# A float32 matmul with bias and residual: row order of the first tiles, paired first loads, the bias by a shuffle, and filler matmuls

## The chip, the core and the metric

The kernel runs on one core of one Trainium2 chip. The core has a matrix engine (TensorE, PE in the profile, with its weight loads as PEld), a vector engine (VectorE, DVE), a scalar engine (ScalarE, ACT), GpSimd (POOL) and a sync engine (SyncE, SP), which here only issues transfers. Sixteen DMA engines carry the transfers between the chip's memory (HBM) and the core's SBUF; each transfer over 128 partitions is split over all sixteen, eight partitions each. The metric is the device time of one execution in microseconds, lower is better.

## The reference

```
x: 16 x 512 x 1024, weight: 1024 x 768, bias: 768, residual: 16 x 512 x 768, all float32
out = matmul(x, weight) + bias + residual
```

Flattened, this is one product of 8192 x 1024 by 1024 x 768. It reads 33.6 MB of x, 25.2 MB of residual and 3.1 MB of weight, and writes 25.2 MB.

## The kernel before, in words

**Tiles and groups.** The 8192 rows are 64 tiles of 128 rows, and four tiles make a group (`G = 4`, 16 groups). A group's rows can lie on the 128 partitions in two ways, which `group` decides. For groups 1 to 15 partition p holds rows 4p to 4p + 3, so that a partition's share of x is one run of 16 KB in memory, and of residual or output one run of 12 KB. For group 0 tile j is rows 128j to 128j + 127, so each row is a run of its own (4 KB of x, 3 KB of residual and output). A row may be in any tile as long as the residual and the output follow the same order, and they do, since all three go through `group`. The weight is kept in two halves of four pieces, and piece k (128 of the 1024 inner rows) is one row per partition, 3 KB.

**One tile.** `cast_x` makes bf16 of the tile, whole on ACT (L124) or, in the first stage, half on ACT (L121) and half on DVE (L122). `transpose` turns its eight 128 x 128 blocks on PE (L140) into a PSUM tile `pt`, `copy_xt` (DVE, L147) brings that to SBUF, `matmul` (L154) makes 16 matmuls, for each of 8 weight pieces one of 512 columns and one of 256, into the PSUM tile `po`. `evacuate` adds: for the first three groups DVE adds the bias into `o_tile` (L169) and POOL adds the residual (L170); later DVE adds the residual in place (L173) and POOL the bias (L175). For the last group the bias is added to the residual ahead of time (`add_bias`, L183). There are three `po` buffers and two `pt` buffers.

**Transfers.** All but the bias are issued by SP, in the order of the program: `load_x` (L96), `load_w` (L101), `load_r` (L105), `store` (L109). At most eight transfers are under way, since eight completion counters go round: each issue waits until the transfer eight places before it has landed. There are four x buffers and a ring of nine buffers shared by weight, residual and output. The bias (one row of 3 KB) is issued by ACT (L81).

**The first stage.** 40 matmuls on a constant tile (`WARM`, L210) come first on PE. Then tiles 0 to 2 are started together, because the weight is still arriving: each weight piece, once it is cast to bf16 (`cast_w`, DVE L131 or ACT L129), is multiplied with all three tiles. The bias is spread to all partitions by a product of a column of ones with the bias row in float32 on PE (L217), copied out by ACT into `bias_bc` (L226). Tile 3 is transposed when the last weight pieces come. The order of issue in this stage is written out by hand, and each engine takes its work in that order (`keep_in_program_order`).

**The loop.** From tile 3 on, each step casts tile t + 3, transposes tile t + 1, multiplies tile t, copies and evacuates. After the last tile of group g SP issues the x and residual of group g + 4 and then the store of group g. The last group is stored in four parts, the last tile as 512 and 256 columns (L285, L288).

Of the kernel before, what the change touches and what calls it, by code (L numbers as in the profile page):

```python
# [8 lines left out]
FP32 = mybir.dt.float32  # L9
BF16 = mybir.dt.bfloat16  # L10
P = 128
G = 4
# [4 lines left out]
PT_BUFS = 2  # L17
PO_BUFS = 3
LATE = 3
WARM = 40  # L20


@with_exitstack
def kernel(
# [8 lines left out]
    nc = tc.nc  # L33
# [4 lines left out]
    N = weight.shape[1]  # L38
# [3 lines left out]
    chunks = [(0, 512), (512, N - 512)]  # L42

    def group(ap, g):
        rows = ap[g * G * P:(g + 1) * G * P, :]


        if g == 0:
            return rows.rearrange("(j p) k -> p j k", p=P)
        return rows.rearrange("(p j) k -> p j k", p=P)  # L50


    w_dram = weight.rearrange("(h p j) n -> h p j n", p=P, j=4)
# [1 line left out]
    const = ctx.enter_context(tc.tile_pool(name="const", bufs=1))  # L55
# [6 lines left out]
    po_pool = ctx.enter_context(  # L62
        tc.tile_pool(name="pop", bufs=1, space=bass.MemoryType.PSUM))

    def o(ins):
        return tc.keep_in_program_order(ins)
# [3 lines left out]
    def slot(pool, base, n, shape, dtype, name=None):  # L70
        i = count.get(base, 0)
        count[base] = i + 1
        return pool.tile(shape, dtype, name=name or base, tag=f"{base}{i % n}", bufs=1)


    warm_in = const.tile([P, P], BF16, name="warm_in")
    o(nc.vector.memset(warm_in, 0.5))  # L77
    ones_row = const.tile([1, P], FP32, name="ones_row")
    o(nc.vector.memset(ones_row, 1.0))
    bias_row = const.tile([1, N], FP32, name="bias_row")  # L80
    o(nc.scalar.dma_start(out=bias_row, in_=bias[None, :]))  # L81
    warm = const.tile([1, 2], FP32, name="warm")
    o(nc.vector.memset(warm, 0.0))
    o(nc.scalar.copy(out=warm, in_=warm))  # L84
# [3 lines left out]
    bias_bc = const.tile([P, N], FP32, name="bias_bc")  # L88
# [4 lines left out]
    def load_x(g, j0=0, j1=G):  # L93
        if g not in x_tiles:
            x_tiles[g] = slot(xin_pool, "x_tile", X_BUFS, [P, G, K], FP32)
        o(nc.sync.dma_start(out=x_tiles[g][:, j0:j1, :], in_=group(x2d, g)[:, j0:j1, :]))  # L96

    def load_w(h, j0, j1):
        if h not in w_stage:
            w_stage[h] = slot(ring_pool, "ring", RING, [P, G, N], FP32, name="w_stage")  # L100
        o(nc.sync.dma_start(out=w_stage[h][:, j0:j1, :], in_=w_dram[h, :, j0:j1, :]))  # L101

    def load_r(g):
        r_tiles[g] = slot(ring_pool, "ring", RING, [P, G, N], FP32, name="r_tile")
        o(nc.sync.dma_start(out=r_tiles[g], in_=group(res2d, g)))  # L105

    def store(g, j0=0, j1=G, n0=0, n1=N):
        src = o_tiles[g] if g < LATE else r_tiles[g]
        o(nc.sync.dma_start(out=group(out2d, g)[:, j0:j1, n0:n1], in_=src[:, j0:j1, n0:n1]))  # L109
# [4 lines left out]
    def cast_x(t, split=False):  # L114
        if t >= n_sub:
            return
        xb_tiles[t] = slot(xb_pool, "xb", XB_BUFS, [P, K], BF16)
        src = x_tiles[t // G][:, t % G, :]
        if split:
            h = K // 2  # L120
            o(nc.scalar.copy(out=xb_tiles[t][:, :h], in_=src[:, :h]))  # L121
            o(nc.vector.tensor_copy(out=xb_tiles[t][:, h:], in_=src[:, h:]))  # L122
        else:
            o(nc.scalar.copy(out=xb_tiles[t], in_=src))  # L124

    def cast_w(k, act=False):
        h, j = divmod(k, 4)
        if act:
            o(nc.scalar.copy(out=w_sb[:, k, :], in_=w_stage[h][:, j, :]))  # L129
        else:  # L130
            o(nc.vector.tensor_copy(out=w_sb[:, k, :], in_=w_stage[h][:, j, :]))  # L131

    def transpose(t):
        if t >= n_sub:
            return
        xb = xb_tiles.pop(t).rearrange("m (h p j) -> m h j p", p=P, j=4)
        pt = slot(pt_pool, "pt", PT_BUFS, [P, n_k, P], BF16)
        for k in range(n_k):
            h, j = divmod(k, 4)
            o(nc.tensor.transpose(out=pt[:, k, :], in_=xb[:, h, j, :], identity=ident))  # L140
        pt_tiles[t] = pt

    def copy_xt(t):
        if t >= n_sub:
            return
        xt_tiles[t] = slot(xt_pool, "xt", XT_BUFS, [P, n_k, P], BF16)
        o(nc.vector.tensor_copy(out=xt_tiles[t], in_=pt_tiles.pop(t)))  # L147

    def matmul(t, k0=0, k1=n_k):
        if t not in po_tiles:  # L150
            po_tiles[t] = slot(po_pool, "po", PO_BUFS, [P, N], FP32)
        for k in range(k0, k1):
            for (n0, nl) in chunks:
                o(nc.tensor.matmul(  # L154
                    po_tiles[t][:, n0:n0 + nl],
                    lhsT=xt_tiles[t][:, k, :],
                    rhs=w_sb[:, k, n0:n0 + nl],
                    start=(k == 0),
                    stop=(k == n_k - 1),
                ))  # L160
# [22 lines left out]
        o(engine.tensor_add(out=rt[:, j, :], in0=rt[:, j, :], in1=bias_bc))  # L183


    load_x(0, 0, 1)
    load_x(0, 1, 2)
    load_w(0, 0, 1)
    load_x(0, 2, 3)
    load_w(0, 1, 2)  # L190
    load_w(0, 2, 3)
    load_w(0, 3, 4)
    load_w(1, 0, 1)
    load_w(1, 1, 2)
    load_w(1, 2, 3)
    load_x(0, 3, 4)
    load_w(1, 3, 4)
    load_x(1, 0, 2)
    load_x(1, 2, 4)
    load_x(2)  # L200
    load_r(0)
    load_x(3)
# [2 lines left out]
    load_r(3)  # L205


    warm_ps = slot(po_pool, "po", PO_BUFS, [P, P], FP32, name="warm_ps")
    for i in range(WARM):
        o(nc.tensor.matmul(warm_ps, lhsT=warm_in, rhs=warm_in, start=True, stop=True))  # L210


    cast_x(0, True)
    transpose(0)
    bias_ps = slot(po_pool, "po", PO_BUFS, [P, N], FP32, name="bias_ps")
    for (n0, nl) in chunks:
        o(nc.tensor.matmul(bias_ps[:, n0:n0 + nl], lhsT=ones_row,  # L217
                           rhs=bias_row[:, n0:n0 + nl], start=True, stop=True))
    slot(po_pool, "po", PO_BUFS, [P, P], FP32, name="unused_ps")
    copy_xt(0)  # L220
    cast_x(1, True)
    transpose(1)
    cast_w(0)
    matmul(0, 0, 1)
    copy_xt(1)
    o(nc.scalar.copy(out=bias_bc, in_=bias_ps))  # L226
    matmul(1, 0, 1)
    cast_x(2, True)
    transpose(2)
# [2 lines left out]
    matmul(0, 1, 2)  # L232
    matmul(1, 1, 2)
    matmul(2, 0, 2)
    for k in range(2, 6):
        cast_w(k, k % 2 == 0)
        for t in range(3):
            matmul(t, k, k + 1)
    cast_w(6)
    cast_x(3, True)  # L240
    transpose(3)
    cast_w(7, True)
    copy_xt(3)
    matmul(0, 6, 7)
    matmul(1, 6, 7)
    matmul(0, 7, 8)
# [9 lines left out]
    for t in range(3, n_sub - 1):  # L256
        g, j = divmod(t, G)
# [24 lines left out]
    for (n0, nl) in chunks:  # L282
        ps = slot(po_pool, "po", PO_BUFS, [P, nl], FP32, name="last_ps")
        for k in range(n_k):
            o(nc.tensor.matmul(ps, lhsT=xt_tiles[t][:, k, :], rhs=w_sb[:, k, n0:n0 + nl],  # L285
                               start=(k == 0), stop=(k == n_k - 1)))
# [31 lines left out]
```

## Time and profile before

| | |
|---|---|
| median of 3 runs | 213.12 us (213.1 to 214.03) |
| the profiled execution | 213.84 us; its span, first to last instruction, 212.1 us |
| PE busy | 202.3 us, 95% of the span |
| DMA queue of SP | 87.04 MB, packets for 97.8% of the time of 16 engines |
| DVE, ACT, POOL busy | 107.4, 65.9, 113.6 us |

Busy times overlap, so their sum means nothing; a busy share of 95% on one engine and of 97.8% on the queue says that both are near their limit, not which of them ends the run. The views used are the page (shares, slices, queues, chain, groups), the waits and the timeline of an engine (start, length, instruction, and in brackets the idle time before it and what ended it), windows (busy time of each engine in a stretch), and the records of the DMA packets (size, start, length of each) and of the completion counters (when each of the sixteen engines reported its part of a transfer), which the trace holds as well.

### The profile page before, as it was taken

The page shows a single profiled execution, that of the slowest core. Times are in us where ns is not written, and L with a number is a line of the kernel's source. Part 1 is how long each engine was busy: PE and PEld are TensorE (multiplying, and loading weights), DVE is VectorE, ACT ScalarE, POOL GpSimd, SP SyncE. Part 2 cuts the span into 40 slices and gives each one's busy share as a digit, 9 for nine tenths or more (in the row PEclk, how much of TensorE's full clock was granted, in tenths as well). Part 3 has the DMA queues.
Part 4 walks back from the last instruction along what each step waited for, and adds up shares of the span by engine and source line. Part 5 has one row for each costly group of instructions (what it writes and reads, how often), then busy time and mean ns, then how long its engine had stood idle before and what let it go on. Part 6 is the DMA issues. An engine that isn't in the chain of part 4 may idle for free.

```text
span 212.1 us, 3712 instructions
## 1 busy us (share of the span) xinstructions
PE 202.3 (95%) x1550; PEld 135.1 (64%) x1580; DVE 107.4 (51%) x143; ACT 65.9 (31%) x70; POOL 113.6 (54%) x68
## 2 busy tenths in 40 slices
PE   8899999999999999999999999999999999999990
PEld 8555666666666666666666666666666666666650
DVE  1556455455545544554455445544554455458750
ACT  3335571411607024070603306070421507042000
POOL 1000009699966556555655565566556655667800
PEclk9889999999999999999999999999999999999998
DMA  6999999999999999999999999999999999999993
GB/s 224 384 414 434 408 429 420 427 430 418 424 428 418 443 420 433 423 431 427 420 432 426 428 426 440 419 425 432 420 432 427 438 416 427 438 414 430 403 401 132
DMA packets 9859, 87.28 MB, mean 412 GB/s; under 512 B 1009, under 2 KB 1137, under 8 KB 4082
## 3 DMA queue, kind: packets, MB, share of 16 engines
q1 hardware_dynamic: 9840, 87.04, 97.8%
q8 instruction: 12, 0.20, 0.4%
q14 instruction: 5, 0.04, 0.0%
q10 hardware_dynamic: 2, 0.00, 0.0%
HBM read 61.87 MB, written 25.17 MB: 410 GB/s over the span
## 4 chain that ended last, share of the span: by engine, by line
PE 90%; DMA 3%; DVE 3%; issue 1%; SPq 0%; DVEq 0%
PE po L154 76%; PE pt L140 13%; DMA w_stage<-in_weight_dram 3%; PE last_ps L285 1%; DVE r_tile L183 1%; DVE xt L147 1%; DVE o_tile L169 0%; SPq L96 0%; DVE w_sb L131 0%; DVE r_tile L288 0%; DVE r_tile L173 0%; DVEq L173 0%; DVEq L169 0%
## 5 line engine op out<-in xcount | busy, mean ns | idle before, releaser
L154 PE MATMUL po<-w_sb,xt 128*128 128x256 bf16 (+1 forms) x978 | 173.1, 325 | 3.0 <-DVE xt L147 0.6
L154 PEld LDWEIGHTS <-xt 128*128 128x128 bf16 x1008 | 96.2, 98 | 60.0 <-DVE xt L147 1.7
L175 POOL TENSOR_TENSOR r_tile<-r_tile,bias_bc 128x768 f32<-128x768 f32 x48 | 88.2, 1838 | 54.8 <-DVE r_tile L173 54.8
L124 ACT CAST xb<-x_tile 128x1024 bf16<-128x1024 f32 x60 | 58.7, 1043 | 115.2 <-DMA x_tile<-in_x_dram 95.3
L173 DVE TENSOR_TENSOR r_tile<-po,r_tile 128x768 f32<-128x768 f32 x51 | 48.8, 957 | 73.6 <-PE po L154 64.3
L147 DVE COPY xt<-pt 128x1024 bf16<-128x1024 bf16 x64 | 43.6, 681 | 4.4 <-PE pt L140 4.4
L140 PEld LDWEIGHTS <-xb 128*128 128x128 bf16 x512 | 35.8, 114 | 8.3 <-ACT xb L121 1.0
L140 PE MATMUL pt<-ident,xb 128*128 128x128 bf16 x512 | 39.6, 221 | 0.0
L170 POOL TENSOR_TENSOR o_tile<-o_tile,r_tile 128x768 f32<-128x768 f32 x12 | 21.4, 1823 | 31.8 <-DMA r_tile<-in_residual_dram 31.8
L169 DVE TENSOR_TENSOR o_tile<-po,bias_bc 128x768 f32<-128x768 f32 x12 | 11.3, 955 | 12.2 <-PE po L154 10.7
L210 PE MATMUL warm_ps<-warm_in 128*128 128x128 bf16 x40 | 4.4, 313 | 1.1 <-DVE warm_in L77 1.1
L210 PEld LDWEIGHTS <-warm_in 128*128 128x128 bf16 x40 | 4.2, 149 | 1.1 <-DVE warm_in L77 1.1
L131 DVE CAST w_sb<-w_stage 128x768 bf16<-128x768 f32 x5 | 2.8, 560 | 3.7 <-DMA w_stage<-in_weight_dram 3.7
L121 ACT CAST xb<-x_tile 128x512 bf16<-128x512 f32 x4 | 2.5, 618 | 5.3 <-DMA x_tile<-in_x_dram 5.3
L122 DVE CAST xb<-x_tile 128x512 bf16<-128x512 f32 x4 | 1.7, 424 | 3.8 <-DMA x_tile<-in_x_dram 3.7
L183 POOL TENSOR_TENSOR r_tile<-r_tile,bias_bc 128x768 f32<-128x768 f32 x2 | 3.6, 1808 | 0.0
L129 ACT CAST w_sb<-w_stage 128x768 bf16<-128x768 f32 x3 | 2.5, 832 | 2.8 <-DMA w_stage<-in_weight_dram 2.8
L183 DVE TENSOR_TENSOR r_tile<-r_tile,bias_bc 128x768 f32<-128x768 f32 x2 | 3.1, 1556 | 0.0
L285 PE MATMUL last_ps<-w_sb,xt 128*128 128x512 bf16 (+1 forms) x16 | 2.8, 326 | 0.0
L285 PEld LDWEIGHTS <-xt 128*128 128x128 bf16 x16 | 1.6, 98 | 1.1
L84 ACT ACT_TABLE_LOAD x1 | 1.3, 1283 | 1.3 <-PEq L302 1.3
L288 DVE TENSOR_TENSOR r_tile<-last_ps,r_tile 128x512 f32<-128x512 f32 (+1 forms) x2 | 1.1, 558 | 0.9 <-PE last_ps L285 0.8
(13 smaller groups left out, 4.5 us busy)
## 6 DMA issues: line engine op xcount, KB each, us to landing
x_tile<-in_x_dram SPq DMA_DIRECT2D x14, 2048.0 KB, 32.8
r_tile<-in_residual_dram SPq DMA_DIRECT2D x16, 1536.0 KB, 32.4
out_dram<-r_tile SPq DMA_DIRECT2D x12, 1536.0 KB, 31.7
out_dram<-o_tile SPq DMA_DIRECT2D x3, 1536.0 KB, 25.8
w_stage<-in_weight_dram SPq DMA_DIRECT2D x8, 384.0 KB, 8.2
x_tile<-in_x_dram SPq DMA_DIRECT2D x4, 512.0 KB, 5.7
x_tile<-in_x_dram SPq DMA_DIRECT2D x2, 1024.0 KB, 10.3
out_dram<-r_tile SPq DMA_DIRECT2D x1, 768.0 KB, 7.5
```

Of the source, the lines that this page charges most:

```text
L124: o(nc.scalar.copy(out=xb_tiles[t], in_=src))
L131: o(nc.vector.tensor_copy(out=w_sb[:, k, :], in_=w_stage[h][:, j, :]))
L140: o(nc.tensor.transpose(out=pt[:, k, :], in_=xb[:, h, j, :], identity=ident))
L147: o(nc.vector.tensor_copy(out=xt_tiles[t], in_=pt_tiles.pop(t)))
L154: o(nc.tensor.matmul(po_tiles[t][:, n0:n0 + nl], lhsT=xt_tiles[t][:, k, :], rhs=w_sb[:, k, n0:n0 + nl], start=(k == 0), stop=(k == n_k - 1),))
L169: o(nc.vector.tensor_add(out=ot[:, j, :], in0=po, in1=bias_bc))
L170: o(nc.gpsimd.tensor_add(out=ot[:, j, :], in0=ot[:, j, :], in1=r_tiles[g][:, j, :]))
L173: o(nc.vector.tensor_add(out=rt, in0=po, in1=rt))
L175: o(nc.gpsimd.tensor_add(out=rt, in0=rt, in1=bias_bc))
L183: o(engine.tensor_add(out=rt[:, j, :], in0=rt[:, j, :], in1=bias_bc))
L210: o(nc.tensor.matmul(warm_ps, lhsT=warm_in, rhs=warm_in, start=True, stop=True))
L285: o(nc.tensor.matmul(ps, lhsT=xt_tiles[t][:, k, :], rhs=w_sb[:, k, n0:n0 + nl], start=(k == 0), stop=(k == n_k - 1)))
```

## The change

Group 0 takes the row order of the other groups. So its x, its residual and its output are runs of 16 KB or 12 KB on a partition, and tiles 0 and 1, and 2 and 3, are loaded as two pairs. Weight pieces 2 and 3, and 4 and 5, are loaded as pairs; group 1 of x is one transfer in place of two. The order of the first transfers is new. The bias row is sent to four partitions (0, 32, 64, 96) of a tile that POOL has set to zero, and a VectorE stream shuffle copies lane 0 of each 32 partitions to all of them; the product with ones and the copy by ACT are gone. Tiles 1 and 3 are cast whole on ACT. Tile 3 is cast, transposed and copied before weight piece 2 is used, no longer after piece 6. `fill(n)` puts n matmuls on the constant tile into PE's order: the 40 at the start, and 10, 6 and 4 more between the first transposes and matmuls; their PSUM tile is the third `po` buffer.

```diff
     def group(ap, g):
-        rows = ap[g * G * P:(g + 1) * G * P, :]
-        if g == 0:
-            return rows.rearrange("(j p) k -> p j k", p=P)
-        return rows.rearrange("(p j) k -> p j k", p=P)
+        return ap[g * G * P:(g + 1) * G * P, :].rearrange("(p j) k -> p j k", p=P)
...
-    ones_row = const.tile([1, P], FP32, name="ones_row")
-    o(nc.vector.memset(ones_row, 1.0))
-    bias_row = const.tile([1, N], FP32, name="bias_row")
-    o(nc.scalar.dma_start(out=bias_row, in_=bias[None, :]))
+    bias_rows = const.tile([P, N], FP32, name="bias_rows")
+    o(nc.gpsimd.memset(bias_rows, 0.0))
+    o(nc.scalar.dma_start(out=bias_rows[0:P:32, :], in_=bias[None, :].to_broadcast([4, N])))
...
-    load_x(0, 0, 1)
-    load_x(0, 1, 2)
+    load_x(0, 0, 2)
     load_w(0, 0, 1)
-    load_x(0, 2, 3)
+    load_x(0, 2, 4)
     load_w(0, 1, 2)
-    load_w(0, 2, 3)
-    load_w(0, 3, 4)
-    load_w(1, 0, 1)
-    load_w(1, 1, 2)
+    load_w(0, 2, 4)
+    load_w(1, 0, 2)
     load_w(1, 2, 3)
-    load_x(0, 3, 4)
     load_w(1, 3, 4)
-    load_x(1, 0, 2)
-    load_x(1, 2, 4)
+    load_x(1)
     load_x(2)
...
-    warm_ps = slot(po_pool, "po", PO_BUFS, [P, P], FP32, name="warm_ps")
-    for i in range(WARM):
-        o(nc.tensor.matmul(warm_ps, lhsT=warm_in, rhs=warm_in, start=True, stop=True))
+    warm_ps = po_pool.tile([P, P], FP32, name="warm_ps", tag="po2", bufs=1)
+    def fill(n):
+        for i in range(n):
+            o(nc.tensor.matmul(warm_ps, lhsT=warm_in, rhs=warm_in, start=True, stop=True))
+    fill(40)
     cast_x(0, True)
     transpose(0)
-    bias_ps = slot(po_pool, "po", PO_BUFS, [P, N], FP32, name="bias_ps")
-    for (n0, nl) in chunks:
-        o(nc.tensor.matmul(bias_ps[:, n0:n0 + nl], lhsT=ones_row,
-                           rhs=bias_row[:, n0:n0 + nl], start=True, stop=True))
-    slot(po_pool, "po", PO_BUFS, [P, P], FP32, name="unused_ps")
+    fill(10)
     copy_xt(0)
-    cast_x(1, True)
+    cast_x(1)
     transpose(1)
+    fill(6)
+    o(nc.vector.stream_shuffle(out=bias_bc, in_=bias_rows, mask=[0] * 32))
     cast_w(0)
     matmul(0, 0, 1)
     copy_xt(1)
-    o(nc.scalar.copy(out=bias_bc, in_=bias_ps))
+    fill(4)
     matmul(1, 0, 1)
     cast_x(2, True)
     transpose(2)
...
     matmul(2, 0, 2)
+    cast_x(3)
+    transpose(3)
+    copy_xt(3)
     for k in range(2, 6):
         cast_w(k, k % 2 == 0)
         for t in range(3):
             matmul(t, k, k + 1)
     cast_w(6)
-    cast_x(3, True)
-    transpose(3)
     cast_w(7, True)
-    copy_xt(3)
     matmul(0, 6, 7)
```

More of the change, by code (lines that the diff above doesn't have):

```diff
@@ L19 @@
 LATE = 3
-WARM = 40
 @with_exitstack
```

## The prediction

> **What bounds the kernel now.** I read the page from the top: engine shares, slices, DMA queues, chain. Two resources come out nearly full, and the page alone does not say which of them ends the run.
>
> ```profile
> PE 202.3 (95%) x1550; PEld 135.1 (64%) x1580; DVE 107.4 (51%) x143; ACT 65.9 (31%) x70; POOL 113.6 (54%) x68
> ...
> PEclk9889999999999999999999999999999999999998
> DMA  6999999999999999999999999999999999999993
> ...
> q1 hardware_dynamic: 9840, 87.04, 97.8%
> q8 instruction: 12, 0.20, 0.4%
> ...
> PE 90%; DMA 3%; DVE 3%; issue 1%; SPq 0%; DVEq 0%
> ```
>
> The chain names PE for 90%, but the one data queue moves packets for 97.8% of the span of all 16 DMA engines, and 0.4% more goes to instruction fetches: 208.3 of 212.1 us on the mean engine. So I looked at who waits for whom at the end, in the timeline of SP's issues, the list of DMA issues and the windows of the tail.
>
> ```profile
> 206.92 0.33 SPq L109 DMA_DIRECT2D out_dram<-r_tile  x1
> ```
>
> ```profile
> out_dram<-r_tile SPq DMA_DIRECT2D x1, 768.0 KB, 7.5
> out_dram<-r_tile SPq DMA_DIRECT2D x1, 384.0 KB, 5.4
> out_dram<-r_tile SPq DMA_DIRECT2D x1, 256.0 KB, 4.5
> out_dram<-r_tile SPq DMA_DIRECT2D x1, 128.0 KB, 4.3
> ```
>
> ```profile
> 199.00:200.00 1.00, 1.00 (x9) 0.61 (x7) 0.41 (x1) 0.00 (x0) 1.00 (x2) 1.00 0.78 332
> 200.00:205.00 5.00, 4.95 (x36) 3.01 (x35) 2.51 (x3) 0.00 (x0) 0.78 (x1) 1.00 0.98 413
> ...
> 207.00:208.00 1.00, 0.00 (x0) 0.00 (x0) 0.00 (x0) 0.00 (x0) 0.00 (x0) 1.00 0.89 345
> 208.00:209.00 1.00, 0.00 (x0) 0.00 (x0) 0.00 (x0) 0.00 (x0) 0.00 (x0) 1.00 0.52 193
> 209.00:210.00 1.00, 0.00 (x0) 0.00 (x0) 0.00 (x0) 0.00 (x0) 0.00 (x0) 1.00 0.23 87
> ```
>
> (Columns of the windows: length, busy PE, PEld, DVE, ACT, POOL, then clock, DMA share, GB/s.) PE is done at 206.4. The last store, 128 KB, is issued at 206.92 and lands 4.3 us later, at 211.2, while the share sinks slowly (0.89, 0.52, 0.23). The DMA engines finish one after another. The landing records of the trace (each of the 16 engines reports its part) say it exactly. The last engine reports the stores of the tail at 203.88, 207.52, 209.34, 210.27, 210.89 and 211.23; these steps of 3.64, 1.82, 0.93, 0.62 and 0.34 are eight packets each at the medians of the packet records (12 KB 460 ns, 6 KB 234, 3 KB 121, 2 KB 84, 1 KB 46: 3.68, 1.87, 0.97, 0.67, 0.37). That engine never waited for data. The end is its backlog, not PE. On the fastest engine the last store landed at 208.59, 1.67 us after issue, and the first load of the run (512 KB, 3.36 us to landing, of which 1.27 is eight 4 KB packets at 159 ns) gives 3.36 - 1.27 + 0.37 = 2.46 us as the other price of a 128 KB store on an empty queue. So PE has 4.3 less 1.67 to 2.46 = 1.8 to 2.6 us of slack at the end.
>
> How near PE is everywhere else shows in the waits of the first stage and the steady state:
>
> ```profile
> 16.49 0.62 ACT L121 CAST xb<-x_tile 128x512 bf16<-128x512 f32 x1 [2.40 <-DMA x_tile<-in_x_dram]
> 17.44 0.83 ACT L129 CAST w_sb<-w_stage 128x768 bf16<-128x768 f32 x1 [0.34 <-DMA w_stage<-in_weight_dram]
> 20.00 1.99 ACT L124 CAST xb<-x_tile 128x1024 bf16<-128x1024 f32 x2 [1.73 <-DMA x_tile<-in_x_dram]
> 22.47 2.00 ACT L124 CAST xb<-x_tile 128x1024 bf16<-128x1024 f32 x2 [0.47 <-DMA x_tile<-in_x_dram]
> ...
> 151.36 3.89 ACT L124 CAST xb<-x_tile 128x1024 bf16<-128x1024 f32 x4 [8.30 <-DMA x_tile<-in_x_dram]
> 163.56 3.89 ACT L124 CAST xb<-x_tile 128x1024 bf16<-128x1024 f32 x4 [8.31 <-DMA x_tile<-in_x_dram]
> ```
>
> Groups of x land every 12.20 us; PE, by the chain, takes 4 x (2.60 + 0.45) = 12.2 us for four tiles; and each first cast of a group ends 2.25 us before its transpose (164.6 against 166.85). PE and DMA run side by side at the same pace, PE a little behind what has landed, the DMA engines never dry.
>
> **The change part by part.**
>
> *Layout, pairs and fewer transfers: DMA time.* This is on the path, since the last DMA engine has no gaps. Each engine moves 8 of a transfer's 128 row pieces; price by the packet medians (also 8 KB 313 ns, 16 KB 611). Tiles of group 0: 32 x 159 = 5.09 becomes 16 x 313 = 5.01. Group 1: 16 x 313 = 5.01 becomes 8 x 611 = 4.89. Weight: 64 x 121 = 7.74 becomes 32 x 121 + 16 x 234 = 7.62. Residual of group 0 and its store, 3 KB pieces now (they too follow the row order): each 32 x 121 = 3.87 becomes 8 x 460 = 3.68. Saved: 0.08 + 0.12 + 0.12 + 0.19 + 0.19 = 0.70. Five transfers fewer (x six to three, weight eight to six), each with a completion write of 9 ns per engine: 0.05. Sum 0.75 us.
>
> The page's list has a transfer landing in 5.7 to 33 us because it stands in a queue, and a transfer's own completion write takes 9 ns. The Trainium skill (DMA: Bandwidth & Descriptors, section "Anatomy of one DMA — SWDGE (gpsimd) path") puts a fixed cost of about 2.0 us on each transfer of the software path; here the hardware path is used, and five fewer would by that rule be 10 us. With the queue full the trace shows none of it, so the rule is left out of the sum.
>
> *Cold packets.* Packets starting before 5 us took 0.60 us per engine more than their medians, those from 5 to 10 us 0.22 us, and the window 4.5 to 6.5 has a DMA share of 0.90, 0.2 us empty. With half as many first packets between 0 and 1.0 us of it could go; between 0 and 0.5 could come, if long packets suffer more. I take 0: it is seen at the first touch of each tensor, which stays.
>
> *First casts, on DVE and ACT.* Tile 0 was cast at 4.12, when its 512 KB had landed, tile 1 at 5.40. Now both come in one transfer: about 5.35. Halves of 0.62 (ACT) and 0.43 (DVE) as before; tiles 1 and 3 are now whole on ACT, 1.04 each, in place of halves.
>
> *Bias.* Removed: two fp32 matmul calls (four recorded, 1.55 us of PE), the copy of 0.80 on ACT. Added: a POOL memset of 128x768 f32; the row 128x128 bf16 took 0.20, six times the columns and twelve times the bytes give 1.2 to 2.4 us. It delays the identity (0.49 on POOL) to 3.6 at most, wanted at 6.0. The bias transfer waits for it on ACT's queue; behind it stand the table load (1.28) and one copy (0.19), done by 5.1 (the issue itself 0.50), before the cast at 5.35. SP's queue is not touched. The shuffle is new; nearest DVE rows of 128x768 are the cast (0.56) and the f32 add (0.95), the dearest 1.56. I take 0.95. It stands before the cast of weight piece 0, which landed at 8.04: DVE idled 0.83 us there. At 1.56 that cast would be 0.7 us later, and pieces 1 to 7 pace PE anyway. It costs nothing on the path. The Trainium skill (VectorE: DVE Perf Modes, "The perf-mode tier table") gives about 2400 ns for a shuffle of 2048 columns, by which mine would be an estimate of 0.9 us.
>
> *Landing order.* By the packet prices, from x0/x1 at 5.35 and weight 0 at 8.0: tiles 2 and 3 at 10.5 (tile 2 was 9.3), weight 1 at 11.5 (10.3), weight 2 and 3 at 13.4 (11.3, 12.25), 4 and 5 at 15.2, 6 at 16.2, 7 at 17.2 (17.4), x of group 1 whole at 22.1 (halves 19.9 and 22.37).
>
> *PE's start.* Weight 2 is cast on ACT until 14.2. Then four weight pieces by three tiles, 0.975 us each: 18.1; pieces 6 and 7, 1.95 us, whose first evacuation (0.97) lets tile 3 start: 20.1; tile 3, 2.6: 22.7. Tile 4 needs group 1: landed 22.1, cast 1.04, transposes 0.45, cast and transposes of tile 5 until 24.6 (copy of tile 4 beside it). Tile 4 starts at 24.6, against 23.93 in the chain: PE is 0.7 us later, although its transposes of tile 3 (0.64) are moved into the wait for weight. From there on the same loop. Price at the end: 0, under the slack of 1.8 to 2.6 (after the DMA gain: 1.1 to 1.9).
>
> *Fillers.* 20 more matmuls. The 40 cost 4.45 us, 0.11 each, at half clock; so at most 2.2 us of PE, in its waits. What they can change is the clock:
>
> ```profile
> 5.84:9.25 3.41, 2.88 (x19) 1.43 (x17) 2.19 (x4) 0.98 (x2) 0.00 (x0) 1.00 0.99 384
> 9.25:12.66 3.41, 3.16 (x15) 1.76 (x17) 2.06 (x4) 1.45 (x2) 0.00 (x0) 0.50 1.03 413
> ```
>
> PE was busy 2.88 of 3.41 us, and the next 3.41 us ran at 0.50. In the changed kernel PE still waits from about 9.8 to 11.2 for tile 2, with no filler there. So a half-speed window of 3.4 us is possible again; a full one costs 1.7 us of PE work. The page TensorE: Matmul & The Clock Gate of the Trainium skill (section "What's actually happening") drops the clock only after an idle window of about 3.4 us. By that rule no gap here, before or after, would do it and the fillers would be worth nothing; the two rows above contradict it, and they decide.
>
> **Sum.** DMA backlog -0.75; PE +0.7, covered. The profiled execution took 213.84 (span 212.1 and 1.74 around it): 213.1. It lay 0.72 above the median of the runs; median 213.12 - 0.75 = 212.4.
>
> **The rivals.**
> 1. *PE takes part of it back* (half-speed window). For: the row above. PE is then 0.7 + 1.7 = 2.4 later. Against a slack that in a median run (0.72 shorter, if by a shorter backlog) is 1.1 to 1.9, the end is 0.5 to 1.3 later than before, less nothing, since the DMA gain is then no longer at the end; a partial window gives zero. 212.8 to 214.4.
> 2. *PE becomes the bound: slower.* Place: the stretch from weight 1 to tile 4. Price: two half-speed windows or a wait of that size, 3.4 us on top of 0.7. It decides once PE is more than 1.1 to 2.6 us late; 4.1 gives 1.5 to 3.0 us more: 214.6 to 216.1. Against: PE has a backlog in that stretch, and a full window (the one at 0.50, 3.16 busy) was followed by 1.00.
> 3. *The start is cleaner than the packet medians say.* The last engine landed weight 0 at 8.04 where the second last had it at 6.72. If bigger pieces take away that lag or the cold extras, 0.5 to 1.3 us more are gained: 211.1 to 211.9. Against: an instruction fetch (16 KB, 1.0 to 1.1 us, twelve of them) can make another engine the last.
> 4. *Nothing happens:* the DMA gain is lost on another engine's fetches: 213.1.
>
> **How the numbers follow.** Forecast 0.46 (212.0 to 212.9); rival 1 and rival 4 together 0.22 (212.8 to 214.4); rival 3 0.19; rival 2 0.13. A measurement can tell about 0.5%, 1.07 us, from no change: faster is under 212.05, slower over 214.19. Faster: rival 3 with the low edge of the forecast, 0.23. Slower: rival 2 and the edge of rival 1, 0.15. Same: 0.62. For 8 in 10 I leave out rival 2 above 214.3 and the last end of rival 3 below 211.4.
>
> **What would show it.** Right: x of group 1 lands near 22, tile 4's matmuls start near 24.6, the queue's share stays above 97%, the first groups' packets are fewer by 1,488 (9840 to about 8350) and the last store still lands over 2 us after its issue. Wrong: the last store lands within 1.7 us of its issue (PE ends the run); a clock of 0.50 over more than one window; weight or x landing earlier or later by over 1 us than listed; a shuffle over 1.6 us.

## The result, and the profile after

| | before | after |
|---|---|---|
| median of 22 runs each, side by side | 213.24 us | 212.91 us |
| ratio after / before | | 0.9977 (0.9966 to 0.9988) |
| profiled execution | 213.84 us, span 212.1 | 212.85 us, span 211.1 |
| packets of SP's queue | 9840 | 8352 |

The ratio is that of the fast runs; one of before's 22 was slow (357.85 us). By it the change is worth 0.49 us (0.26 to 0.73). The medians are closer, 0.33 us apart: three of before's other 21 executions took 214.0 us or more, and none of the changed kernel's 22 did (the highest is 213.37). Without those three the means differ by 0.36 us. A second measurement of the same kernel, further down, gave 0.9969 (0.9952 to 0.9986), 0.66 us; there nine of before's 23 took 214.0 or more and none of the changed kernel's 12, and without the nine the means differ by 0.34 us. So a part of the gain is that the longest executions of before are gone, and how many there are differs from series to series. The median stands 0.5 us above the forecast of 212.4, inside the whole range but at the upper edge of the forecast's own band (212.0 to 212.9); 0.1 of it is before itself, 213.24 here and 213.12 in the prediction.

The page of the changed kernel, same parts as before:

```profile
PE 202.3 (96%) x1596; PEld 134.7 (64%) x1596; DVE 107.0 (51%) x142; ACT 66.0 (31%) x69; POOL 114.5 (54%) x69
...
PEclk9999999999999999999999999999999999999999
DMA  6999999999999999999999999999999999999895
...
q1 hardware_dynamic: 8352, 87.04, 97.9%
q8 instruction: 12, 0.20, 0.4%
```

PE has the same busy time and the queue the same bytes; two things differ. The clock digits are all 9, so the half-speed window of before is gone. And the DMA row ends in 8, 9, 5 where it ended in 9, 9, 3: the queue now has a thin place ahead of the last store. The tail in SP's timeline, the DMA list and the windows (columns as before):

```profile
207.51 0.33 SPq L103 DMA_DIRECT2D out_dram<-r_tile  x1
```

```profile
out_dram<-r_tile SPq DMA_DIRECT2D x1, 128.0 KB, 2.5
```

```profile
199.00:200.00 1.00, 1.00 (x8) 0.61 (x7) 1.00 (x2) 0.00 (x0) 1.00 (x2) 1.00 0.58 246
...
207.00:208.00 1.00, 0.02 (x1) 0.00 (x0) 0.42 (x1) 0.00 (x0) 0.00 (x0) 1.00 0.62 245
208.00:209.00 1.00, 0.00 (x0) 0.00 (x0) 0.00 (x0) 0.00 (x0) 0.00 (x0) 1.00 0.92 336
209.00:210.00 1.00, 0.00 (x0) 0.00 (x0) 0.00 (x0) 0.00 (x0) 0.00 (x0) 1.00 0.09 31
```

The last store is issued at 207.51, 0.6 us later than before, and lands 2.5 us after, at 210.0; before it took 4.3 us and landed at 211.2. So both sides moved, towards each other: the backlog shrank by 1.2 us in this execution and PE came 0.6 us later. Before, the window from 209 to 210 still had a share of 0.23; now it is 0.09. The slowest DMA engine still had no gap (it reported its last parts in steps of 3.66, 1.81, 0.93, 0.63 and 0.33 us, its packets back to back), but the mean share of the sixteen was 0.58 from 199 to 200 and 0.62 from 207 to 208, so the faster ones ran dry there.

PE at the start of tile 4, before and after (timeline of PE):

```profile
22.54 1.06 PE L140 MATMUL pt<-ident,xb 128*128 128x128 bf16 x16
23.93 2.77 PE L154 MATMUL po<-w_sb,xt 128*128 128x512 bf16 x16 [0.34 <-DVE xt L147]
```

```profile
23.11 0.64 PE L134 MATMUL pt<-ident,xb 128*128 128x128 bf16 x8 [0.77 <-ACT xb L118]
24.06 0.64 PE L134 MATMUL pt<-ident,xb 128*128 128x128 bf16 x8 [0.31 <-ACT xb L118]
24.53 2.67 PE L148 MATMUL po<-w_sb,xt 128*128 128x512 bf16 x15
```

The brackets tell the new wait: PE stands idle until ACT has cast tiles 4 and 5, and ACT's cast waits for group 1, which is one transfer now:

```profile
22.01 3.89 ACT L118 CAST xb<-x_tile 128x1024 bf16<-128x1024 f32 x4 [4.11 <-DMA x_tile<-in_x_dram]
```

### The profile page after: what moved, and what is told of

Read it like the earlier page. It is cut to its first block, busy times and chain, and to the rows that moved or that the text cites. A ratio compares the mean times of both kernels' runs of the same rounds, so it can differ in the third digit from the quotient of the medians.

```text
span 211.1 us, 3768 instructions
## 1 busy us (share of the span) xinstructions
PE 202.3 (96%) x1596; PEld 134.7 (64%) x1596; DVE 107.0 (51%) x142; ACT 66.0 (31%) x69; POOL 114.5 (54%) x69
## 3 DMA queue, kind: packets, MB, share of 16 engines
q1 hardware_dynamic: 8352, 87.04, 97.9%
## 4 chain that ended last, share of the span: by engine, by line
PE 85%; DMA 10%; DVE 2%; issue 1%; ACT 1%; POOL 0%; ACTq 0%; DVEq 0%; POOLq 0%
PE po L148 72%; PE pt L134 12%; DMA x_tile<-in_x_dram 7%; DMA bias_rows<-in_bias_dram 3%; PE last_ps L275 1%; DVE r_tile L177 1%; ACT xb L118 1%; DVE xt L141 0%; DVE r_tile L278 0%; POOL ident masks.py:197 0%; ACTq L118 0%; POOL bias_rows L74 0%; DVE r_tile L167 0%; DVEq L167 0%; POOLq L292 0%
## 5 line engine op out<-in xcount | busy, mean ns | idle before, releaser
L148 PE MATMUL po<-w_sb,xt 128*128 128x512 bf16 x1008 | 174.6, 326 | 1.2 <-DVE w_sb L125 0.8
L118 ACT CAST xb<-x_tile 128x1024 bf16<-128x1024 f32 x62 | 61.0, 1043 | 115.2 <-DMA x_tile<-in_x_dram 109.2
L134 PE MATMUL pt<-ident,xb 128*128 128x128 bf16 x512 | 39.1, 219 | 2.4 <-ACT xb L115 1.3
L201 PE MATMUL warm_ps<-warm_in 128*128 128x128 bf16 x60 | 6.1, 282 | 1.1 <-DVE warm L77 1.1
L201 PEld LDWEIGHTS <-warm_in 128*128 128x128 bf16 x60 | 5.5, 132 | 1.2 <-DVE warm L77 1.1
L177 POOL TENSOR_TENSOR r_tile<-r_tile,bias_bc 128x768 f32<-128x768 f32 x2 | 3.6, 1804 | 0.0
L116 DVE CAST xb<-x_tile 128x512 bf16<-128x512 f32 x2 | 0.8, 423 | 5.2 <-DMA x_tile<-in_x_dram 5.2
L177 DVE TENSOR_TENSOR r_tile<-r_tile,bias_bc 128x768 f32<-128x768 f32 x2 | 3.1, 1551 | 0.0
L115 ACT CAST xb<-x_tile 128x512 bf16<-128x512 f32 x2 | 1.2, 618 | 3.9 <-DMA x_tile<-in_x_dram 3.9
```

Of the source, the lines that this page charges most:

```text
L148: o(nc.tensor.matmul(po_tiles[t][:, n0:n0 + nl], lhsT=xt_tiles[t][:, k, :], rhs=w_sb[:, k, n0:n0 + nl], start=(k == 0), stop=(k == n_k - 1),))
```

## The experiments

Theory A is the prediction's: the backlog of the last DMA engine ends the run, so packet time taken out is gained, as long as PE stays within its slack. Times below are ratios to the kernel before, measured beside each run, turned into microseconds with its 213.2. The changed kernel was beside none but its own, so differences between a run and it are indirect. The diffs are shortened: lines in plain words stand for code, and `...` for what is left out.

**1. The transfers alone**

```diff
+ group(): (p j) for all groups
+ the changed list of first loads (pairs, group 1 whole)
  (bias product, split casts, PE's order, 40 fillers: as before)
```

> The kernel before with the transfer part of the change alone (row order of group 0, the pairs, the new order of the first loads); bias product, split casts, and PE order as before, no fillers. Theory A (the backlog of the last DMA engine ends the run, and the change gained by taking 0.75 us of packet time out of it): the packet time of the SP queue falls by 0.7 to 0.8 us per engine, and the time by 0.4 to 0.8 us against the kernel before, as in the changed kernel. Rival B (the gain comes from PE: the warm clock and the shorter first stage): 0.0, or slower by up to 1 us, since tile 0 starts 1 to 2 us later.

1.0005 (0.9983 to 1.0028), +0.1 us. A miss for theory A: the packet time fell to 206.64 us per engine (207.41 before, 206.62 in the changed kernel), as it said, and the ratio shows no gain. The time is the one that rival B named. In the profile PE was as late as in the changed kernel (last store issued at 207.53) and had a window at clock 0.50 from 8.4 to 11.9 us. Of twelve runs nine lay between 213.0 and 213.7, three at 214.7 to 215.0. The three weigh on the ratio: the median, 213.33, is 0.2 us under that of before beside it, 213.55.

**2. The transfers undone**

```diff
+ group 0 as (j p); single tiles and weight pieces, group 1 in halves
  (the changed order of loads; shuffle, fillers and PE's order as changed)
```

> The changed kernel with the transfers as before (row order of group 0, single tiles, single weight pieces, group 1 in halves), but in the changed order. Theory A: packet time as before, 207.4 us per engine, and the time of the kernel before, -0.2 to +0.2 us. Rival B: the gain stays, -0.4 to -0.6 us against before.

0.9996 (0.9981 to 1.0011), packet time 207.49: no gain, as theory A has it. Rival B falls: the profile had the clock at 1.00 all through the work, and that alone is worth nothing that can be measured. But run 1 says the same of the transfers alone. Neither half shows the gain by itself, though the intervals reach to -0.4 us in both, into that of the whole change (-0.26 to -0.73).

**3. Group 1 in halves**

```diff
-    load_x(1)
+    load_x(1, 0, 2)
+    load_x(1, 2, 4)
```

> The changed kernel, but group 1 of x comes in two halves as before. Packet time +0.12 us per engine; tile 4 should start at about 23.5 instead of 24.5 us and the last store be issued 1 us earlier. Theory A alone: 0.1 us slower than the changed kernel (-0.4 us against before). Rival P (in the changed kernel PE, 0.6 us later than before, gives part of the gain back in the usual run): 0.2 to 0.4 us faster than the changed kernel, -0.7 to -0.9 us against before.

Tile 4 starts at 23.38, 1.15 us earlier, as expected, but the last store is issued at 206.99, only 0.5 earlier; 0.9981 (0.9968 to 0.9994), -0.4 us. The time is that of theory A; the other 0.6 us of PE's lead were lost at the end of the loop. So rival P had only half of its condition here, and run 8 takes it up again. DVE's timeline there:

```profile
190.72 0.96 DVE L167 TENSOR_TENSOR r_tile<-po,r_tile 128x768 f32<-128x768 f32 x1 [1.49 <-PE po L148]
192.50 1.88 DVE L177 TENSOR_TENSOR r_tile<-r_tile,bias_bc 128x768 f32<-128x768 f32 x1 [0.82 <-DMA r_tile<-in_residual_dram]
194.30 0.68 DVE L141 COPY xt<-pt 128x1024 bf16<-128x1024 bf16 x1
```

L177 is `add_bias` on the last group's residual. It waits 0.82 us for that residual to land, and behind it in DVE's order stands the copy that PE needs for its next tile. So PE, once it is early, is held here by the queue.

**4. Without the later fillers**

```diff
-    fill(10)
...
-    fill(6)
...
-    fill(4)
```

> The changed kernel without the 10, 6 and 4 fillers behind the first transposes. If the fillers keep the clock: a window at 0.50 of 3.4 us between 9 and 16 us, tile 4 up to 1.7 us later, and against the changed kernel 0 (if covered) to +1.3 us. If they do nothing: clock 1.00 and the time of the changed kernel, within 0.2 us.

A window at 0.50 came, from 8.8 to 12.2 us:

```profile
8.80:12.20 3.40, 2.62 (x14) 1.66 (x15) 2.51 (x6) 1.57 (x2) 0.00 (x0) 0.50 1.03 427
```

Tile 4 started at 24.81 instead of 24.53, and the last store was issued 0.28 us later. 0.9991 (0.9976 to 1.0006): between before and changed, apart from neither. In this one profile the clock fell without the fillers, as expected; that they save time is not shown.

**5 and 6. PE 1.94 us later in the middle, in both kernels**

```diff
+ if t == 32:  nine matmuls of 512 columns into po_tiles[32], then its product from the start
```

> The kernel before with nine extra 512-column matmuls ahead of tile 32's product (their sum is started anew after them, the output is unchanged): 9 x 0.216 = 1.94 us of PE in the middle of the loop, no transfer touched. Theory A (PE had 1.1 to 1.9 us of slack at the end in a usual run, 1.8 to 2.6 in the profiled one): the last store is issued at about 208.9 instead of 206.9, and the time grows by 0 to 0.8 us. Rival B (PE sets the end): it grows by 1.9 us.

> The same 1.94 us of extra matmuls in the changed kernel. There the last store landed 2.49 us after its issue, and the fastest engine took 1.68: slack 0 to 0.8 us. Expected: 1.1 to 1.9 us slower than the changed kernel, that is +0.6 to +1.5 us against the kernel before. If PE still had the slack of before, 0 to 0.8 us slower than the changed kernel, at or under the time of before.

Before: 1.0019 (1.0005 to 1.0032), +0.4 us. Of 1.94 us PE's slack took 1.5. (The profiled execution is one of its longer ones, 214.51 us: there tile 4 already started at 25.13, 1.2 us later than in the profile of before, and the last store was issued at 210.05 and not at 208.9.) Changed: 1.0024 (1.0011 to 1.0037), +0.5 us over before, so 1.0 to 1.2 us over the changed kernel, by either of its two measurements; its slack took only 0.7 to 0.9. In both profiles PE ends the run: the last store lands 1.85 us (before) and 1.86 us (changed) after its issue, with no queue ahead of it. The two issues:

```profile
210.05 0.33 SPq L109 DMA_DIRECT2D out_dram<-r_tile  x1
```

```profile
209.35 0.33 SPq L103 DMA_DIRECT2D out_dram<-r_tile  x1
```

That is a better price for an empty queue than the 1.67 to 2.46 of the prediction. With it the slack in the profiled executions is 4.31 - 1.86 = 2.5 us before and 2.49 - 1.86 = 0.6 us after.

**7. 3.68 us of packets less, PE's work the same**

```diff
-        o(nc.sync.dma_start(out=r_tiles[g], in_=group(res2d, g)))
+        if g != 9:
+            o(nc.sync.dma_start(out=r_tiles[g], in_=group(res2d, g)))
...
-            o(nc.vector.tensor_add(out=rt, in0=po, in1=rt))
+            o(nc.vector.tensor_add(out=rt, in0=po, in1=bias_bc if g == 9 else rt))
```

> The kernel before, but the residual of group 9 is not loaded and not added (its four tiles add the bias twice instead, with the same instructions), so PE, DVE and POOL do the same work and the queue has 1.57 MB or 3.68 us per engine less. Theory A: the time falls until PE ends the run: by 1.1 to 1.9 us, and not by 3.7; the last store then lands within 1.7 to 2.5 us of its issue. Rival B (PE sets the end): 0 to -0.3 us.

0.9897 (0.9876 to 0.9919), -2.2 us (1.7 to 2.6), a little more than the 1.1 to 1.9 expected and far from 3.7: the gain stops where PE takes over. The list of issues has the last store's landing at PE's price:

```profile
out_dram<-r_tile SPq DMA_DIRECT2D x1, 128.0 KB, 1.9
```

Before was bound by the queue, and PE stood some 2 us behind.

**8. PE earlier at the end of the loop**

```diff
  (on top of run 3; add_bias takes the engine and the columns now)
         if g == n_grp - 2 and j >= 2:
-            add_bias(n_sub - G + 2 * (j - 2))
-            add_bias(n_sub - G + 2 * (j - 2) + 1)
+            add_bias(n_sub - G, nc.vector, (j - 2) * (N // 2), (j - 1) * (N // 2))
+            if j == 3:
+                for i in range(1, G):
+                    add_bias(n_sub - G + i, nc.gpsimd)
```

> The changed kernel with group 1 of x in halves, and the bias of the last group's residual added otherwise: DVE adds it to tile 60 in two halves (one in each of two steps), POOL to tiles 61, 62 and 63 after its own last additions. In the run with halves alone PE came 1.2 us earlier than in the changed kernel until tile 58, and lost 0.7 us of it in the last group, where DVE, with the copy for PE queued behind it, waited 0.82 us for the last residual and then worked beside POOL at half its rate. Expected: last store issued at 205.9 to 206.4 instead of 207.0, and, if in the changed kernel PE gave part of the gain back, 0.2 to 0.5 us faster than the changed kernel, -0.7 to -1.0 us against before. If only the DMA backlog counts: -0.4 us against before, as the changed kernel.

The last store is issued at 206.11, 1.4 us before that of the changed kernel, and lands 4.2 us later, at 210.3:

```profile
206.11 0.33 SPq L103 DMA_DIRECT2D out_dram<-r_tile  x1
```

0.9987 (0.9971 to 1.0004), -0.3 us: PE's 1.4 us bring nothing. The slack is back and unused; the backlog ends the run. So PE's 0.6 us do not explain why the changed kernel gained less than 0.75, and rival P falls.

**9 to 11. What packet time is worth**

```diff
  changed kernel, measured again
```

> The changed kernel once more, beside the two price runs, since its gain of 0.49 us (0.26 to 0.73) just misses the 0.75 us of packet time that were taken away. Theory A (all of it reaches the end): -0.5 to -0.9 us against before. Rival H (part of it does not): -0.2 to -0.5 us.

```diff
+ tile 39's residual is not loaded (the bias is added in its place)
```

> The kernel before, but tile 39 (the last of group 9) gets the bias in place of its residual, which is not loaded: a quarter of that transfer less, 0.9 us per engine, within the slack that PE has (about 2 us by the two delay and cut runs). Theory A: 0.7 to 1.1 us faster than before. Rival H (part of a saving is lost whatever its kind): 0.3 to 0.6 us faster.

```diff
-        if g == 0:
+        if g >= 0:
             return rows.rearrange("(j p) k -> p j k", p=P)
```

> The kernel before with the row order of group 0 for all sixteen groups: same bytes, pieces of 3 KB in place of 12 for residual and output, of 4 KB (8 in group 1 no more) in place of 16 for x. By the packet medians 15 x (0.19 + 0.19) + 14 x 0.20 + 0.08 = 8.6 us more per engine. Theory A: the time grows by 8 to 9 us. Rival H: by 4 to 6 us.

Again: 0.9969 (0.9952 to 0.9986), -0.66 us; that lies in theory A's range, but the interval, 0.3 to 1.0 us, reaches through that of rival H. A quarter transfer less, 0.90 us by the medians (eight packets of 460 ns become eight of 348): 0.9954 (0.9933 to 0.9975), -1.0 us (0.5 to 1.4), by its middle value all of it gained. Small pieces everywhere, 8.6 us more by the medians: 1.0309 (1.0274 to 1.0344), +6.6 us (5.8 to 7.3): between the two theories. By these two runs a saving in bytes reaches the end whole, and a change in the number of pieces less than its packet records say. The steady state shows why; the first window is of the kernel before, the second of this run:

```profile
60.00:180.00 120.00, 119.06 (x933) 79.84 (x950) 61.59 (x80) 38.89 (x40) 70.57 (x40) 1.00 1.01 427
```

```profile
60.00:180.00 120.00, 117.30 (x918) 76.82 (x916) 59.42 (x76) 34.99 (x36) 69.66 (x39) 1.00 1.03 413
```

The share is the sum of packet lengths over time and engines. With small pieces it is 1.03: the records of successive packets overlap by some 2% more, so that the median length of a small packet (121 ns) is more than what it takes from the queue. The landings say how much. On the last engine x, residual and store of a group step by 4.88, 3.65 and 3.66 us before, and by 5.06, 3.82 and 3.75 with small pieces: differences of 0.18, 0.17 and 0.09, where the medians gave 0.20, 0.19 and 0.19. The store's was priced at twice its worth. 15 x (0.17 + 0.09) + 14 x 0.18 + 0.1 = 6.5 us, against 6.6 measured.

**12. The transfers alone, group 1 in halves**

```diff
  (run 1, with load_x(1, 0, 2) and load_x(1, 2, 4))
```

> The kernel before with the transfers alone changed, and group 1 of x in halves as before. The run with the transfers alone showed no gain (1.0005, 0.9983 to 1.0028) although its profile had the shorter packet time; there PE was 0.6 us later than before and had a window at half clock. If PE's lateness took the gain in its usual run, it comes back here, where tile 4 starts about 0.5 to 1 us earlier: -0.4 to -0.7 us against before, and a last store issued near 207.0. If the transfers alone gain nothing for another cause: -0.1 to +0.1 us.

0.9987 (0.9969 to 1.0004), -0.3 us: between the two. The profiled execution, 213.27 us, had two windows in a row at half clock,

```profile
8.40:11.80 3.40, 3.25 (x19) 1.76 (x18) 1.85 (x4) 1.32 (x2) 0.00 (x0) 0.50 1.02 417
11.80:15.20 3.40, 3.18 (x15) 1.77 (x14) 1.84 (x4) 1.94 (x3) 0.00 (x0) 0.50 1.03 418
```

and tile 4, which should have come early, started at 25.56, 1.6 us later than in the kernel before:

```profile
25.56 2.66 PE L150 MATMUL po<-w_sb,xt 128*128 128x512 bf16 x15 [0.34 <-DVE xt L143]
```

```profile
208.54 0.33 SPq L105 DMA_DIRECT2D out_dram<-r_tile  x1
```

That store landed at 210.39, 1.85 us later: PE ended this run. The queue would have let it end earlier. So with the lighter queue PE's slack is small, and a second window at half clock can use it up. But this does not explain the long executions of runs 1 and 12. The mean granted clock is on record for every execution, and the profiled one with its two windows has 0.984. In run 12 the six executions at 0.984 took 213.11 to 213.33 us, and the two at 0.999 and 1.000 took 213.71 and 214.71. In run 1 the five at 0.984 took 213.24 to 213.30, and the three longest, 214.71 to 215.02, were at 1.000, which leaves no room for a window at half clock. What makes them long stays open, since none of them has a profile, and with it why the transfers alone show no gain.

Over all profiles: the six with the later fillers (the changed kernel twice, runs 2, 3, 6 and 8) ran the first stage at 1.00. Of the eight without them, seven had a window at 0.50 (before, runs 1, 4, 5, 7, 12, and the one without part of group 9's residual); the run with small pieces everywhere had none. The mean clocks of all executions, which also hold a stretch at half clock after PE's last work, point the same way without proving it: the changed kernel's 34 have 0.992 to 1.000, and eight of run 4's twelve 0.990 or less; but one execution each of runs 2 and 3, with the fillers, has 0.983 and 0.985.

No version that does the whole work was faster than the changed kernel beyond the intervals.

## Why the prediction was right or wrong, point by point

**What bounds it: right.** The backlog ends the run, PE has slack. Shown from both sides: 1.94 us more of PE cost 0.4 us, and 3.68 us less of packets gained 2.2. The slack of "1.8 to 2.6" measured 2.5 in the profiled execution, and about 1.5 to 2.2 over all runs. All the signs named for "right" came: group 1 at 22.0, tile 4 at 24.53, a share of 97.9%, 8352 packets, a last store that lands 2.5 us after its issue.

**The DMA term: right mechanism, size probably too large.** The sum said -0.75. Its step "each 32 x 121 = 3.87 becomes 8 x 460 = 3.68" priced 3 KB pieces at their median record length. Records of small packets overlap; by the landing steps of the run with small pieces everywhere the residual is worth 0.17 instead of 0.19 and the store 0.09 instead of 0.19, and the 4 KB pieces of x a tenth less. With those: 0.07 + 0.12 + 0.12 + 0.17 + 0.09 + 0.05 = 0.62 us. The two measurements have 0.49 and 0.66. (The weight's 3 KB and 6 KB pieces keep the medians here; they had no run of their own.) The times alone do not tell 0.62 from 0.75: the first interval ends at 0.73, the second reaches from 0.3 to 1.0. And run 1, with the same packet time taken out, shows no gain, so that the term reaches the end is shown for the change as a whole only.

**Cold packets at 0:** the packets that start before 10 us took 0.67 us more than their medians, 0.82 before. 0.15 us went, within the bounds given; one execution each, and not in the 0.62.

**Landing order: shape and end right, the rest off by 0.8 to 1.0 us.** The first pair landed at 6.13, not 5.35, and weight 0 at 7.20, not 8.0. Tiles 2 and 3 at 9.6 (10.5 predicted), weight 1 at 10.5 (11.5), the pairs at 12.4 and 14.3 (13.4 and 15.2), weight 6 at 15.3 (16.2), weight 7 at 17.05 (17.2), group 1 at 22.0 (22.1). The lag of one engine that the prediction carried over from weight 0 in the profile of before did not come again. It changed nothing, because group 1's landing is what counts for PE.

**PE's start: right.** Tile 4 at 24.53, predicted 24.6, and the reason is the predicted one, the wait for group 1 as one transfer. The cover held: 0.6 us later at the last store, at no price. What the prediction did not draw from its own numbers (1.1 to 1.9 us of slack after the DMA gain, less 0.7) is that the cover is nearly used up: 0.6 us of slack are left, and the delay of 1.94 us that cost 0.4 before cost 1.0 to 1.2 now.

**The bias: right in effect, sizes off at one end.** The memset took 0.74 us, not 1.2 to 2.4; the nearest row had far fewer columns and a fixed part. The shuffle took 1.01 (taken: 0.95). The estimate of 0.9 from the Trainium skill (VectorE: DVE Perf Modes, "The perf-mode tier table") is 0.1 under it. The cast of weight 0 had to wait for the shuffle: the weight landed at 7.20, the cast began at 9.01, and PE stood 0.82 us for the cast, in the stretch that the wait for group 1 covers.

**The fillers and the clock.** The prediction set the trace's row against the rule of the Trainium skill of an idle window of about 3.4 us (TensorE: Matmul & The Clock Gate, "What's actually happening") and let the row decide. The runs agree with the row: in the seven profiles with a window at 0.50, PE's longest gap in the 3.41 us before it was 0.3 to 1.3 us. But the busy share that the prediction quoted, 2.88 of 3.41 us, is not what decides: the changed kernel's window at the same place is less busy and kept the full clock.

```profile
5.84:9.25 3.41, 1.98 (x32) 1.86 (x33) 2.18 (x5) 1.57 (x2) 0.00 (x0) 1.00 1.01 420
9.25:12.66 3.41, 3.03 (x25) 1.86 (x25) 2.50 (x5) 1.78 (x3) 0.00 (x0) 1.00 1.04 432
```

Of the 2.88 us of before, 1.4 are the float32 bias product, on a single row of the array, which the change takes out. That this work does not count for the clock would fit the two windows and is not shown: no run changed it alone, and run 4, which has no such product, lost the clock after a window with 1.37 us busy. The 20 later fillers took 1.6 us together, under the 2.2 allowed. Rival 1 was right in kind, and was placed in the wrong kernel: neither profile of the changed one has the half clock, and it was seen in the transfers without the rest.

**The rivals.** Rival 2 (PE the bound, slower) did not happen. Rival 3 needed more than 1.2 us. Rival 4 is excluded by the interval. "Within 0.5%" was the likeliest class, and the measured -0.23% and -0.31% lie in it.

## What to carry to other kernels

Where two resources are almost full, ask for each how much could be added before the end moves, and read it from the last transfer: the time from its issue to its landing, less the same on an empty queue, is the slack of the engines before it. A gain on the bound is only kept while the other resource stays inside that slack, so a saving on the queue has to be measured together with what it does to PE: here the transfers alone and the rest alone showed no gain (+0.1 and -0.1 us), both together gained 0.5 to 0.7, and the runs leave open why the transfers alone did not. Price small DMA pieces by the steps between landings on a full queue and not by packet record lengths.

## What the runs showed that was not expected

- Packet records of 3 and 4 KB pieces overlap on a full queue: the share reads 1.03 where it reads 1.01 with 12 and 16 KB pieces, and a group's store in 3 KB pieces costs each engine 0.09 us more than in 12 KB pieces instead of the 0.19 of the medians.
- PE's clock: take the first full window at clock 1.00 of each profile and leave the one-row float32 matmuls out of the busy time. In the seven profiles whose next window was at 0.50 it was 0.95 to 1.66 us of 3.41; in the seven that kept the clock 1.82 to 2.69. A later window of 1.43 us in run 2 kept it too, and in run 12 a window of 2.75 us, itself at 0.50, was followed by a second one at 0.50; so this is an order in the numbers and not yet a rule. No run changed the bias product alone.
- Two f32 additions of 128x768 from SBUF to SBUF, one on DVE and one on POOL, hold each other up. In the kernel before, L183 on DVE took 0.95 us when it began first and POOL's L175, 0.16 us behind, took 2.47 instead of 1.81; when POOL had begun 0.46 us earlier, DVE took 2.16.
- PE's lead over the queue is cut at one instruction: of 1.15 us won at tile 4 in run 3, 0.6 were gone by the last store, because DVE's bias addition waits for the last residual with PE's copy behind it.
- On an empty queue the last 128 KB store lands 1.85 to 1.9 us after its issue, alike in four runs (5, 6, 7 and 12).
